# Moving the weight-block additions of the seven-product scheme from the vector engine to GpSimd

## Chip, cores and metric

The kernel runs on one core of one Trainium2 chip. The metric is the device time of one execution in microseconds (us).

## The reference, cut to what matters

Two network blocks work on 512 tokens of width 1024 in float32: a first block of two layers and a second block of one layer. What the change touches is the wide half of each feed-forward part (w_ff1 twice, then w_up):

```python
# first block, two layers
x = x + jnp.square(jax.nn.relu(h @ w_ff1[l])) @ w_ff2[l]     # 1024 -> 4096 -> 1024
# second block
f = jnp.square(jax.nn.relu(h @ w_up)) @ w_down
```

Around these stand pooling, latent attention and a recurrent branch (first block) and a state-space branch and dilated attention (second block); the change doesn't touch them.

## The kernel before

**Precision.** A float32 operand is split into a high and a low part in the fast matmul format: ACT copies the source to `hi`, DVE subtracts `lo = src - hi` (`split`). A product is then three matmuls (`mm3`): high x high, high x low, low x high.

**Seven products in place of eight.** For a pair of output tiles (128 columns each) of the wide projection, `up` (from L613 on) computes a 2 x 2 block product with seven block products in place of eight. A pair is called a unit here. Its weight blocks come from `wforms`: it loads two raw panels of 128 x 1024 (`r1`, `r2`, class W), whose halves are the blocks a11, a22, a12, a21 of 128 x 512, and forms four sums with the helper `add`: s1 = a22 + a21, s2 = s1 + a11, s3 = a11 + a21 and s2 + a12. Three blocks and the four sums are split by `both` into high and low (seven tiles of class W). The sums are tiles of class T, so in the trace the additions are `T<-W,W` (s1, s3) and `T<-T,W` (s2, s2 + a12). The activations' sums are made once per stage by `xforms`.

One product is four blocks of 128 rows times three matmuls of 256 columns, so a unit has 84 matmuls. `up` adds several products into the same PSUM tile `a`, and copies the tile out between them: product 0, copy, product 5, copy, product 6, copy, product 3, copy. Products 1, 4 and 2 go to two other PSUM tiles and fill the time of the copies. Afterwards DVE squares the positive part and the result is split.

**Loops.** `ffn` runs four units first; then for each of 24 panels of the down projection (each 24 matmuls of 512 columns) it does one unit after every second panel; the last eight panels follow. There are 16 units in each of the first block's two feed-forward stages and 14 in the second block's, 46 in all.

**What sets the order.** The kernel records every operation (`record`) with a duration from `cost`, and a list planner (`order`) lays all of them out over the five engines with the tile slots: 57 of class T, 16 of class W, 8 of PSUM. The instructions are then issued in this order, each engine in its own. Operations that write a W tile have 250 places of priority (`LEAD`). The planner may swap some ACT and DVE copies (`other`); it has no other engine for a GpSimd operation. Its prices for an addition of n elements a row are

```python
d = 65 + per * N + 60 * (ptr > 0)                             # vector, per = 1.05
d = 80 + (2.15 if m != "memset" else 0.9) * n(a[0])           # gpsimd
```

Since all instructions are issued from the one line of `emit`, L505 stands on every row of the profile; rows are told apart by engine, operation and tiles. `self.G` is needed for the activations' sums (a list, set in `mix1` and `out2`), and hides the proxy of the same name.

Of the kernel before, what the change touches and what calls it, by code (L numbers as in the profile page):

```python
# [11 lines left out]
ALU = mybir.AluOpType  # L12
# [49 lines left out]
class View:  # L62
    def __init__(self, tile, ops=()):
        self.tile, self.ops = tile, ops
# [122 lines left out]
class Recorder:  # L187
# [2 lines left out]

    def __init__(self, tc):
        self.tc, self.nc = tc, tc.nc
        self.V, self.A, self.G, self.E, self.S = (Proxy(self, e) for e in ("vector", "scalar", "gpsimd", "tensor", "sync"))
        self.ops = []


# [316 lines left out]
class Net(Recorder):  # L513
# [36 lines left out]
    def wforms(self, name, p):  # L550


        V, off, w = self.V, WOFF[name][0], 1024
        r1, r2 = self.new("W", w), self.new("W", w)
        for i, t in enumerate((r1, r2)):
            self.S.dma_start(t, bass.AP(tensor=self.wp.tensor, offset=off + (2 * p + i) * P * w, ap=[[w, P], [1, w]]))
        L, R = slice(0, T), slice(T, w)

        def both(x):
            hl = self.new("W", w, F32R)  # L560
            self.split(x, hl[:, L], hl[:, R])
            return hl[:, L], hl[:, R]

        def add(a, b):
            o = self.F()
            V.tensor_tensor(o, a, b, op=ALU.add)
            return o

        a11, a22, a12, a21 = r1[:, L], r1[:, R], r2[:, L], r2[:, R]
        f11, f12 = both(a11), both(a12)  # L570
        s1 = add(a22, a21)
        s2 = add(s1, a11)
        g2, g1 = both(s2), both(s1)
        s3 = add(a11, a21)
        g3, f22 = both(s3), both(a22)
        return f11, f12, both(add(s2, a12)), f22, g1, g2, g3
# [1192 lines left out]
```

## Time and profile before

| | us |
|---|---|
| median of 2 runs | 2489.48 (2489.26 to 2489.7) |
| the profiled execution's own time | 2488.91 |
| its span, first to last instruction | 2487.1 |

PE is TensorE's matmuls, PEld its weight loads, DVE the vector engine, ACT the scalar engine, POOL GpSimd, SP the engine that issues the transfers. A row of a group of instructions shows the engine, the operation, the tiles written and read, the shapes and the number, then the busy time, the mean length of one in ns, and how long the engine had been idle before them, with what ended that. The three feed-forward stages lie at about 326 to 720, 1026 to 1400 and 2112 to 2456 us of the span. TensorE's granted clock is at the full 2.4 GHz level in all three but for a few us.

### The profile page before, as it was taken

To read this page: it belongs to the slowest core of one execution; us is meant where nothing else is said; L and a number is where in the kernel's file an instruction comes from. 1 tells how busy PE (TensorE), PEld (TensorE's weight loads), DVE (VectorE), ACT (ScalarE), POOL (GpSimd) and SP (SyncE) were. 2 spreads that over 40 slices of the span, in tenths; PEclk is the share of its full clock that TensorE was granted. 3 is DMA by queue.
4 is the path that set the end of the run, shared out by engine and by line. 5 is a ranking of instruction groups with operands and counts; after the bars stand their busy time and mean duration, and the time that the engine had idled before them with its cause. 6 is when DMAs were issued, how large, how long until landed. Compare 5 with 4: busy or idle time off the path is not lost.

```text
span 2487.1 us, 35399 instructions
## 1 busy us (share of the span) xinstructions
PE 2462.5 (99%) x13822; PEld 2098.7 (84%) x13822; DVE 1911.1 (77%) x3451; ACT 1157.8 (47%) x2067; POOL 0.2 (0%) x4
## 2 busy tenths in 40 slices
PE   8999999999999999999999999999999999999997
PEld 7888889899888888899999977777778789998897
DVE  7868578777778785797776757588999887987775
ACT  5555355333345463553333334356755752743332
POOL 0000000000000000000000000000000000000000
PEclk9999999999999999999999999999999999999998
DMA  4222333333422223333333322244433452233321
GB/s 177 66 78 91 127 119 113 92 105 116 150 88 86 70 94 120 117 118 99 100 114 115 109 71 68 89 138 127 127 94 115 122 181 66 81 116 102 102 94 35
DMA packets 88599, 260.59 MB, mean 105 GB/s; under 512 B 10032, under 2 KB 13232, under 8 KB 88432
## 3 DMA queue, kind: packets, MB, share of 16 engines
q1 hardware_dynamic: 88432, 258.34, 32.6%
q8 instruction: 108, 1.77, 0.3%
q14 instruction: 59, 0.48, 0.1%
HBM read 245.59 MB, written 12.71 MB: 104 GB/s over the span
## 4 chain that ended last, share of the span: by engine, by line
PE 98%; DVE 1%; ACT 1%; issue 0%; DMA 0%; SPq 0%; ACTq 0%; DVEq 0%
PE P L505 98%; DVE T L505 1%; ACT T L505 1%; DMA T<-in_x_dram 0%; DVE W L505 0%; ACT W L505 0%; DVE S L505 0%; DVE xl L505 0%; SPq L505 0%; ACTq L1765 0%; ACT xh L505 0%; DVE xh L505 0%; DVEq L505 0%; ACTq L505 0%
## 5 line engine op out<-in xcount | busy, mean ns | idle before, releaser
L505 PE MATMUL P<-T,W 128*128 128x512 f32 (+1 forms) x5580 | 1100.2, 349 | 2.0 <-ACT T L505 2.0
L505 PE MATMUL P<-xh,W 128*128 128x512 f32 (+1 forms) x3912 | 1064.8, 351 | 8.1 <-DVE xh L505 6.3
L505 PEld LDWEIGHTS P<-T,W 128*128 128x128 f32 x5580 | 894.6, 188 | 142.5 <-ACT T L505 2.9
L505 PEld LDWEIGHTS P<-xh,W 128*128 128x128 f32 x3912 | 681.6, 189 | 114.1 <-issue 12.2
L505 PE MATMUL P<-xl,W 128*128 128x512 f32 (+1 forms) x1968 | 685.6, 351 | 1.2 <-DVE xl L505 1.2
L505 DVE TENSOR_TENSOR W<-W,W 128x1024 fp32r<-128x1024 f32 (+2 forms) x441 | 460.1, 1046 | 250.3 <-PE P L505 126.6
L505 ACT ACTIVATE W<-W 128x1024 fp32r<-128x1024 f32 (+2 forms) x424 | 386.8, 915 | 548.8 <-PE P L505 492.0
L505 PEld LDWEIGHTS P<-xl,W 128*128 128x128 f32 x1968 | 371.3, 189 | 55.6 <-issue 5.5
L505 DVE TENSOR_TENSOR T<-T,T 128x512 f32<-128x512 f32 (+6 forms) x636 | 378.9, 614 | 23.8 <-ACT T L505 14.1
L505 ACT ACTIVATE T<-T 128x512 fp32r<-128x512 f32 (+5 forms) x365 | 207.5, 578 | 250.2 <-DVE T L505 240.3
L505 PE MATMUL P<-T,T 128*128 128x256 f32 (+7 forms) x1536 | 278.0, 311 | 0.1
L505 PEld LDWEIGHTS P<-T,T 128*128 128x128 f32 (+2 forms) x1536 | 211.0, 184 | 39.8 <-issue 19.8
L505 ACT ACTIVATE T<-P 128x256 f32<-128x256 f32 (+7 forms) x295 | 136.6, 486 | 220.2 <-PE P L505 219.4
L505 DVE TENSOR_TENSOR T<-T,P 128x256 f32<-128x256 f32 (+2 forms) x328 | 166.7, 510 | 81.1 <-PE P L505 67.3
L505 DVE TENSOR_TENSOR T<-P,T 128x512 f32<-128x512 f32 (+5 forms) x224 | 131.1, 612 | 28.6 <-PE P L505 22.0
L505 ACT ACTIVATE W<-T 128x512 fp32r<-128x512 f32 x159 | 100.0, 631 | 110.1 <-PE P L505 96.3
L505 DVE TENSOR_TENSOR W<-T,W 128x512 fp32r<-128x512 f32 x184 | 124.0, 687 | 11.4 <-ACT W L505 9.5
L505 ACT ACTIVATE T<-T,T 128x128 f32<-128x128 f32 (+1 forms) x320 | 122.8, 455 | 7.9 <-DMA T<-fscr 6.7
L505 DVE SCALAR_TENSOR_TENSOR T<-T,P 128x512 f32<-128x512 f32 (+1 forms) x120 | 67.5, 575 | 38.8 <-PE P L505 27.3
L505 DVE COPY T<-P 128x256 f32<-128x256 f32 (+2 forms) x121 | 59.4, 493 | 30.1 <-PE P L505 28.6
L505 PE MATMUL P<-c,T 128*128 128x128 f32 (+1 forms) x436 | 75.1, 272 | 0.2 <-DVE T L505 0.2
L505 DVE SCALAR_TENSOR_TENSOR T<-P,half,T 128x510 f32<-128x510 f32 (+1 forms) x96 | 69.9, 743 | 0.4
(80 smaller groups left out, 1046.5 us busy)
## 6 DMA issues: line engine op xcount, KB each, us to landing
W<-in_w_dram SPq DMA_DIRECT2D x382, 512.0 KB, 3.6
T<-fscr SPq DMA_DIRECT2D x64, 256.0 KB, 4.6
T<-in_w_dram SPq DMA_DIRECT2D x24, 256.0 KB, 4.7
T<-in_x_dram SPq DMA_DIRECT2D x16, 256.0 KB, 5.6
rscr<-T SPq DMA_DIRECT2D x16, 256.0 KB, 3.9
T<-rscr SPq DMA_DIRECT2D x16, 256.0 KB, 5.2
W<-in_w_dram SPq DMA_DIRECT2D x10, 384.0 KB, 3.4
T<-in_c_dram SPq DMA_DIRECT2D x8, 256.0 KB, 4.0
```

The source lines that it names most:

```text
L505: self.out(o, getattr(getattr(self.nc, o.eng), o.meth)(*[res(a) for a in o.args], **{k: res(v) for k, v in o.kw.items()}))
```

## The change

The helper `add` of `wforms` records its addition on GpSimd in place of the vector engine. The GpSimd proxy gets the name `G_`, since `G` is taken over by the list named above. The planner is run with its price for GpSimd, so the order of instructions and the slots may change everywhere behind the first addition.

```diff
-        self.V, self.A, self.G, self.E, self.S = (Proxy(self, e) for e in ("vector", "scalar", "gpsimd", "tensor", "sync"))
+        self.V, self.A, self.G_, self.E, self.S = (Proxy(self, e) for e in ("vector", "scalar", "gpsimd", "tensor", "sync"))
...
         def add(a, b):
             o = self.F()
-            V.tensor_tensor(o, a, b, op=ALU.add)
+            self.G_.tensor_tensor(o, a, b, op=ALU.add)
             return o
```

## Rows read from the trace of the kernel before

**Rows 1.** The page, busy us (share of the span) x instructions of each engine.

```profile
PE 2462.5 (99%) x13822; PEld 2098.7 (84%) x13822; DVE 1911.1 (77%) x3451; ACT 1157.8 (47%) x2067; POOL 0.2 (0%) x4
```

**Rows 2.** Stretches: length, busy us (instructions) of PE, PEld, DVE, ACT, POOL; clock, DMA.

```profile
326.00:720.00 394.00, 394.00 (x2384) 349.75 (x2383) 303.12 (x497) 169.19 (x273) 0.00 (x0) 1.00 0.37 116
...
1026.00:1400.00 374.00, 374.00 (x2514) 343.42 (x2512) 293.01 (x542) 157.68 (x263) 0.00 (x0) 1.00 0.35 111
...
2112.00:2456.00 344.00, 340.20 (x2330) 313.99 (x2330) 265.77 (x494) 146.04 (x265) 0.00 (x0) 1.00 0.28 89
2456.00:2487.10 31.10, 18.14 (x129) 17.09 (x127) 17.97 (x61) 9.98 (x25) 0.00 (x0) 0.75 0.20 68
...
364.00:411.00 47.00, 47.00 (x385) 46.00 (x384) 44.51 (x84) 29.52 (x56) 0.00 (x0) 1.00 0.40 119
```

**Rows 3.** Waits of PE, 2112 to 2456 us: us in total, times, longest.

```profile
PE P L505 <- ACT T L505: 2.0, 1, 2.0
```

**Rows 4.** Groups of instructions on DVE, whole span: the additions, and the slowest operation.

```profile
L505 DVE TENSOR_TENSOR T<-T,W 128x512 f32<-128x512 f32 x92 | 62.9, 684 | 0.1
...
L505 DVE TENSOR_TENSOR T<-W,W 128x512 f32<-128x512 f32 x92 | 61.4, 683 | 0.6 <-DMA W<-in_w_dram 0.6
...
L505 DVE RECIPROCAL T<-T 128x512 f32<-128x512 f32 x4 | 13.4, 3340 | 0.0
```

**Rows 5.** Groups: additions from 326 to 396 us, 256-column matmuls from 326 to 409.6.

```profile
L505 DVE TENSOR_TENSOR T<-T,W 128x512 f32<-128x512 f32 x10 | 6.8, 684 | 0.0
L505 DVE TENSOR_TENSOR T<-W,W 128x512 f32<-128x512 f32 x10 | 6.6, 683 | 0.0
...
L505 PE MATMUL P<-xh,W 128*128 128x256 f32 x128 | 23.3, 277 | 0.0
L505 PE MATMUL P<-T,W 128*128 128x256 f32 x144 | 19.4, 283 | 0.0
L505 PE MATMUL P<-xl,W 128*128 128x256 f32 x64 | 17.6, 277 | 0.0
```

**Rows 6.** DVE: groups of 432.02 to 453.02 us, then single instructions (start, length).

```profile
L505 DVE TENSOR_TENSOR W<-T,W 128x512 fp32r<-128x512 f32 x4 | 2.7, 688 | 0.0
L505 DVE TENSOR_TENSOR W<-W,W 128x1024 fp32r<-128x1024 f32 x2 | 2.5, 1226 | 4.2 <-issue 3.9 <-PE P L505 0.4
L505 DVE TENSOR_TENSOR W<-W,W 128x512 fp32r<-128x512 f32 x3 | 2.1, 690 | 0.3 <-ACT W L505 0.2
...
L505 DVE TENSOR_TENSOR T<-T,T 128x512 fp32r<-128x512 f32 x2 | 1.4, 684 | 0.0
...
L505 DVE SCALAR_TENSOR_TENSOR T<-T 128x512 f32<-128x512 f32 x2 | 1.4, 683 | 0.0
...
395.06 0.69 DVE L505 TENSOR_TENSOR T<-T,W 128x512 f32<-128x512 f32 x1
...
436.52 0.41 DVE L505 COPY T<-P 128x256 f32<-128x256 f32 x1
...
439.53 0.42 DVE L505 COPY T<-P 128x256 f32<-128x256 f32 x1
...
448.88 0.69 DVE L505 TENSOR_TENSOR T<-T,W 128x512 f32<-128x512 f32 x1
```

**Rows 7.** PE in order of time: start us, length us, what, how many.

```profile
409.70 0.28 PE L505 MATMUL P<-xh,W 128*128 128x256 f32 x1
...
432.02 0.28 PE L505 MATMUL P<-xh,W 128*128 128x256 f32 x1
...
434.85 1.58 PE L505 MATMUL P<-T,W 128*128 128x256 f32 x12
...
437.64 1.59 PE L505 MATMUL P<-T,W 128*128 128x256 f32 x12
...
440.23 0.50 PE L505 MATMUL P<-T,W 128*128 128x512 f32 x2
...
453.02 0.28 PE L505 MATMUL P<-xh,W 128*128 128x256 f32 x1
```

## The prediction

> **What bounds the kernel.** I read the page's busy times first, then the stretches by stage, then what TensorE waited for, and at the end one period of the feed-forward loop instruction by instruction. PE is busy for 2462.5 of 2487.1 us [rows 1], so it has 24.6 us of idle time in the whole span. The stretches say where it lies: 13.0 us after 2456 us, 3.8 us in the third feed-forward stage (2112 to 2456), and none in the first two (326 to 720 and 1026 to 1400), where PE is busy for every microsecond [rows 2]; the remaining 7.8 us are outside these stages. The longest wait in the third stage is 2.0 us, for an ACT result [rows 3]. "Busy" is modelled, so I looked at the pace too: in the loop two products begin at 434.85 and 437.64 us [rows 7], and the 24 matmuls of 256 columns between these two points take 0.116 us each, with no hole. PE streams at its pace. All 184 additions that the change moves lie in these three stages, so what the vector engine saves there can shorten nothing but the 3.8 us. DVE is at 303.12 of 394, 293.01 of 374 and 265.77 of 344 us in them, 77 to 78%: loaded, and not what ends.
>
> **The change, part by part.**
>
> *Renaming the proxy.* It emits no instruction: nothing used the GpSimd proxy before (POOL holds four memsets, 0.2 us [rows 1]). Price nothing. The planner has no other engine for a GpSimd operation, so all 184 additions do go there; that the change does nothing is not a rival.
>
> *What leaves DVE.* There are 46 units of seven products (16, 16 and 14 per stage), each with four additions: 92 that read two W tiles (61.4 us) and 92 that read a T and a W tile (62.9 us) [rows 4]. That is 124.3 us, 0.676 us each. DVE falls to 303.12 - 64 x 0.676 = 259.9 us in the first stage, 293.01 - 43.3 = 249.7 in the second and 265.77 - 56 x 0.676 = 227.9 in the third. It saves time only where PE waited on DVE: at most the 3.8 us of the third stage, and those waits hang on the layer normalisation and on ACT; I take 0.
>
> *What comes to GpSimd.* No GpSimd arithmetic is in the trace of before. From below one addition costs no less than DVE's 0.676 us; from above the slowest element-wise operation of this size in the trace is the DVE reciprocal, 3.34 us [rows 4]. I take 1.18 us, which is what the kernel's own planner writes down for it (80 + 2.15 x 512 ns); it is nearer the adder's row than the reciprocal's, as an addition should be. Then GpSimd works 4 x 1.18 = 4.7 us in a unit. A unit with two panels of the down projection takes 21.0 us (units start at 432.02 and 453.02 [rows 7]), so GpSimd alone keeps up, even at 3.34 us (13.4 us).
>
> *Is the sum late?* What waits for an addition is the split of its result: the copy on ACT and the subtraction on DVE. Behind these stand, in order on their engines, the copies out of PSUM, and PE waits for those. So I count how early the additions are. From 326 to 396 us there are 20 of them, those of five units [rows 5], the last beginning at 395.06 [rows 6]; PE has by 409.6 done 128 + 144 + 64 = 336 matmuls of 256 columns, exactly four units of 84 [rows 5], and begins the fifth at 409.70 [rows 7]. The tightest unit thus has its last sum 409.70 - 395.75 = 13.95 us before its first product. In the loop it is more: the additions that end at 449.57 [rows 6] are for the unit after the one that starts at 453.02, at 474.0, 24 us later. Each unit's chain is three sums long at most, so at 1.18 us it is later by about 3 x (1.18 - 0.676) = 1.5 us and at 3.34 by 8.0 us. Both fit under 13.95. The new waits (GpSimd for the panel's transfer, GpSimd for its own last result, ACT and DVE for GpSimd) thus cost nothing as long as the lead stands; if a later order had no lead, a unit would lose 1.5 us, 46 x 1.5 = 69 us in all. The two raw panels stay in their slots 1.5 us longer. SyncE's issues are the same in number and size, no DMA is moved, and nothing else queues on POOL.
>
> *Do the two engines hinder each other?* Nearly all of DVE's work in the loop has both inputs in SBUF: in one period the splits and squares take 2.7 + 2.5 + 2.1 + 1.4 + 1.4 = 10.1 us [rows 6] beside the additions. No run here shows an addition of GpSimd beside them, so I bound it. Without hindrance the price is 0. If the two work strictly one after the other, 64 additions and DVE's rest need 259.9 + 64 x 1.18 = 335.4 us of the first stage's 394, 325.2 of 374 in the second and 294.0 of 344 in the third: still less than PE takes. The densest stretch, 364 to 411 us, where DVE has 44.51 of 47 us [rows 2], would need, with 16 additions for the four units that PE does in it, 44.51 - 16 x 0.68 + 16 x 1.18 = 52.5 us, 5.5 us too many, less than the lead of 13.95. So PE stays the bound at this price. The Trainium skill states this hindrance outright and it speaks against the change: "SBUF — State Buffer" (Who interferes with whom) says that a DVE instruction with two SBUF inputs and a GpSimd instruction that reads SBUF share a read interface, and that the second to be issued waits until the first is done. "GPSIMD Engine Reference" (Performance versus the Vector engine) measures such an addition at 4497 ns for 2048 elements against 2293 on DVE and advises DVE; a quarter, 1124 ns, would be an estimate for ours, and the three sums above would fall by 3 to 4 us each. No run here shows either yet.
>
> *The hand-offs.* A unit adds several products into one PSUM tile, with a copy out between them. After the product that begins at 434.85 [rows 7], DVE copies from 436.52 to 436.93 [rows 6] and PE goes on in that tile at 437.64 [rows 7]: 0.71 us to spare. The next copy ends at 439.95 [rows 6]; PE goes on with the second of the two matmuls of the row at 440.23, about 440.23 + 0.50 - 0.28 = 440.45 [rows 7]: 0.50 to spare. If DVE is held up by one addition, up to 1.18 us, PE loses up to 0.47 and 0.68 us. GpSimd is busy for 4.7 of 21 us, 22%; with the hold-up spread evenly from 0 to 1.18 the mean excess is 0.47 x 0.47 / 2.36 + 0.68 x 0.68 / 2.36 = 0.29 us, times 0.22 times 46 = 2.9 us. I take 2.9.
>
> *A new order.* The planner lays out every instruction anew with the new costs. PE's work stays the same, so I take 0 with a few us either way.
>
> **The sum.** 2487.1 + 2.9 = 2490.0 us of span; the profiled run took 2488.91 us, 1.8 us beyond its span, so 2491.8 us. The profiled run is 0.57 us under the median of 2489.48, so I round to 2492. Its own range is 2484 to 2500.
>
> **The rivals.**
> - *The hand-offs are hit every time.* If the plan repeats itself from period to period, an addition can stand in front of the copies in all of them: 46 x (0.47 + 0.68) = 52.9 us, 2542. For it: the loop's units follow each other in an even period of 21.0 us [rows 7], so a bad place comes back. Against it: DVE loses four instructions and already sits idle for 4.2 us ahead of one split in the period [rows 6]. The case covers 2500 to 2539.
> - *The vector engine becomes the bound, kernel slower.* It needs additions that hold DVE up for more than (394 - 259.9) / 64 = 2.10, (374 - 249.7) / 64 = 1.94 and (344 - 227.9) / 56 = 2.07 us. At 3.34 the stages would grow by 79.7, 89.5 and 70.9 us: 2489 + 240 = 2729. Below 1.94 us it costs nothing.
> - *A gain.* DVE's relief closes the 3.8 us of the third stage and the order turns out lucky: 2485, hardly under 2480. The last 13.0 us lie behind the last unit, in the layer normalisation of the output.
>
> **How the numbers follow.** Forecast 0.77 (2484 to 2500), hand-offs 0.12 (2500 to 2539), DVE bound 0.06 (2540 to 2729), gain 0.05 (2480 to 2485). A change of 2%, 49.8 us, is about what a measurement of this kernel can tell from none. Faster by more than that would need twice PE's idle time; I leave 0.01 for what I don't see, out of the gain's. Slower has the 0.06, the rest 0.93. A range of 2482 to 2512 leaves out the DVE bound, about half of the gain and two thirds of the hand-off case: 0.06 + 0.02 + 0.08 = 0.16.
>
> **What the profile after would show.** Right: POOL busy 184 x 1.2 = about 220 us, PE's busy time and pace unchanged, DVE's total at 1787 us or stretched by waits, no new wait of PE from 326 to 1400. The hand-off case: PE waiting on DVE T or ACT T inside the units, up to 0.7 us at a time, in every period. The DVE bound: additions of 2 us or more, DVE instructions longer than their 0.68 us, and stages longer than 394 and 374 us. My lead argument is wrong if PE waits for W tiles.

## The result and the profile after

| | before | after |
|---|---|---|
| median of 2 runs, us | 2489.48 | 2574.48 (2571.6 to 2577.36) |
| ratio to before, 95% interval | | 1.0344 [1.0326, 1.0362] |
| profiled run, us | 2488.91 | 2571.6 |
| its span, us | 2487.1 | 2569.8 |

The kernel became 3.4% slower. The span grew by 82.7 us; the prediction had said 2492 us and a range up to 2512.

The page of after, in the columns of [rows 1]:

```profile
PE 2496.8 (97%) x13822; PEld 2120.9 (83%) x13822; DVE 1953.9 (76%) x3303; ACT 1135.5 (44%) x2031; POOL 292.5 (11%) x188
```

The 184 additions are on POOL. DVE lost them and is nevertheless busier than before, 1953.9 against 1911.1 us [rows 1]. It has 3303 instructions, not 3451 - 184 = 3267: ACT lost 36 (2067 to 2031) and DVE got 36, so the planner moved copies onto the engine that it thought relieved. PE does the same 13822 matmuls; it is idle for 2569.8 - 2496.8 = 73.0 us, 48.4 more than the 24.6 of before.

The groups of instructions of after tell why DVE is busy (busy us, mean ns of one, then the idle time before them):

```profile
L505 POOL TENSOR_TENSOR T<-W,W 128x512 f32<-128x512 f32 x92 | 147.1, 1619 | 2125.7 <-DMA W<-in_w_dram 1136.3 <-ACT T L505 862.5 <-DVE T L505 77.2
...
L505 POOL TENSOR_TENSOR T<-T,W 128x512 f32<-128x512 f32 x92 | 146.9, 1597 | 35.1 <-DVE T L505 14.9 <-PE P L505 11.2 <-DVE W L505 5.7
...
L505 DVE TENSOR_TENSOR W<-T,W 128x512 fp32r<-128x512 f32 x184 | 150.6, 825 | 10.5 <-ACT W L505 8.8
...
L505 DVE TENSOR_TENSOR T<-T,P 128x256 f32<-128x256 f32 x218 | 89.8, 415 | 54.5 <-PE P L505 50.0 <-ACT T L505 2.6
```

An addition takes 1.61 us on GpSimd. The splits on DVE (W<-T,W, both inputs in SBUF) take 825 ns on average where they took 688 in [rows 6]. The operation with one input from PSUM (T<-T,P) takes 415 ns, as it did.

The list of one tile's instructions gives the spread of the additions (shortest, median, longest, ns):

```profile
L505 POOL TENSOR_TENSOR T<-W,W x92: 1282/1423/6641, 327.8 to 2448.2; 128x512 f32<-128x512 f32 x92
L505 POOL TENSOR_TENSOR T<-T,W x92: 1278/1616/2278, 330.5 to 2452.0; 128x512 f32<-128x512 f32 x92
```

Fourteen additions ran beside no DVE operation with two SBUF inputs, and these took 1.29 us each: that is the price with nothing in the way. The longest took 6.64 us (at 2210.66 us). During it DVE did nine operations in a row at their usual lengths, so here it was GpSimd that waited.

The stretches of after, start of each feed-forward stage and its loop, in the columns of [rows 2]:

```profile
326.00:440.00 114.00, 106.83 (x652) 96.15 (x651) 99.77 (x150) 55.82 (x100) 37.51 (x24) 0.96 0.29 90
440.00:740.00 300.00, 294.45 (x1716) 257.95 (x1715) 215.30 (x298) 101.38 (x152) 61.18 (x40) 0.99 0.38 118
1040.00:1160.00 120.00, 111.91 (x675) 100.34 (x674) 104.53 (x151) 55.03 (x101) 45.91 (x28) 0.96 0.32 102
1160.00:1450.00 290.00, 287.06 (x1932) 264.01 (x1932) 217.29 (x366) 105.48 (x171) 56.09 (x36) 0.99 0.33 105
2130.00:2260.00 130.00, 116.12 (x850) 108.83 (x849) 106.57 (x214) 59.89 (x130) 36.55 (x20) 0.96 0.24 78
2260.00:2500.00 240.00, 225.98 (x1386) 201.19 (x1385) 169.71 (x232) 80.05 (x126) 55.03 (x36) 0.98 0.29 92
```

PE now has holes in all of them: 7.2, 8.1 and 13.9 us in the starts (length less PE's busy time) and 5.6, 2.9 and 14.0 us in the loops, where before had none in the first two stages and 3.8 us in the third [rows 2]. In the third loop they come in every unit: PE waits for an ACT result at 2268.5, 2313.9, 2360.9, 2406.5 and 2453.5 us (1.8 to 2.1 us each) and for a DVE result at 2288.3, 2335.1, 2380.8 and 2427.7 (0.9 to 1.1).

Some waits in the whole span of after, of PE and, last, of ACT for a sum (us in total, times, longest):

```profile
PE P L505 <- ACT T L505: 25.3, 14, 2.8
PE P L505 <- DVE T L505: 13.1, 14, 2.2
PE P L505 <- DVE xl L505: 7.3, 7, 2.3
PE P L505 <- ACT W L505: 2.9, 1, 2.9
ACT W L505 <- POOL T L505: 6.3, 2, 3.9
```

PE waits for ACT and DVE results of class T (copies out of PSUM, activations) and for the low parts of the activations (xl). It waits for ACT's split of a weight panel once, 2.9 us at 2210 us; write_only and order_only below show the same wait, so it belongs to the new order. The sums come in time with two exceptions, both behind the addition of 6.64 us: ACT waits 6.3 us for them, and a wait of PE of 2.18 us follows at 2223 us.

**One hold-up, instruction by instruction.** The timeline of after from 395 to 404 us (start, length, engine, what; in brackets the idle time before it and what ended it):

```profile
395.11 3.00 POOL L505 TENSOR_TENSOR T<-W,W 128x512 f32<-128x512 f32 x2 [19.45 <-DMA W<-in_w_dram]
395.70 1.25 DVE L505 SCALAR_TENSOR_TENSOR T<-T 128x512 f32<-128x512 f32 x1
...
396.87 1.78 DVE L505 TENSOR_TENSOR W<-T,W 128x512 fp32r<-128x512 f32 x1
...
398.06 3.42 POOL L505 TENSOR_TENSOR T<-T,W 128x512 f32<-128x512 f32 x2
...
398.57 0.41 DVE L505 TENSOR_TENSOR T<-T,P 128x256 f32<-128x256 f32 x1
...
398.90 1.44 DVE L505 TENSOR_TENSOR T<-T,T 128x512 fp32r<-128x512 f32 x1
...
400.27 1.75 DVE L505 SCALAR_TENSOR_TENSOR T<-T 128x512 f32<-128x512 f32 x1
...
402.06 0.63 ACT L505 ACTIVATE T<-T 128x512 fp32r<-128x512 f32 x1 [3.44 <-DVE T L505]
...
402.60 0.61 ACT L505 ACTIVATE W<-W 128x512 fp32r<-128x512 f32 x1
...
403.12 0.36 ACT L505 ACTIVATE T<-P 128x256 f32<-128x256 f32 x1
...
403.53 1.83 PE L505 MATMUL P<-T,W 128*128 128x256 f32 x7 [2.81 <-ACT T L505]
```

This shows how the hold-up reaches PE. GpSimd does a unit's four additions in one burst, 395.11 to 401.48. In that time DVE does four operations with SBUF inputs. They take 1.25 + 1.78 + 1.44 + 1.75 = 6.2 us in place of 4 x 0.68 = 2.7; only the one that reads PSUM keeps its 0.41. Here the two engines take turns, one instruction each. DVE's square is late, so ACT stands for 3.44 us before its split of it; behind that split stand, in ACT's order, another split and the copy of a PSUM tile; and PE waits 2.81 us for that copy. The hold-up of a neighbour arrived two engines away, through the order of ACT's queue.

### The profile page after: what moved, and what is told of

Its sections match the earlier page's. It is cut to its first block, busy times and chain, and to the rows that moved or that the text cites. A ratio compares the mean times of both kernels' runs of the same rounds, so it can differ in the third digit from the quotient of the medians.

```text
span 2569.8 us, 35772 instructions
## 1 busy us (share of the span) xinstructions
PE 2496.8 (97%) x13822; PEld 2120.9 (83%) x13822; DVE 1953.9 (76%) x3303; ACT 1135.5 (44%) x2031; POOL 292.5 (11%) x188
## 3 DMA queue, kind: packets, MB, share of 16 engines
q8 instruction: 108, 1.77, 0.3%
## 4 chain that ended last, share of the span: by engine, by line
PE 51%; DVE 3%; issue 1%; ACT 1%; DMA 0%; POOL 0%; SPq 0%; ACTq 0%; DVEq 0%; POOLq 0%
PE P L505 51%; DVE W L505 2%; DVE T L505 2%; ACT T L505 0%; DMA W<-in_w_dram 0%; DVE S L505 0%; ACT W L505 0%; DVE xl L505 0%; POOL T L505 0%; SPq L505 0%; DVEq L505 0%; ACTq L1765 0%; ACTq L505 0%; POOLq L505 0%
## 5 line engine op out<-in xcount | busy, mean ns | idle before, releaser
L505 PE MATMUL P<-T,W 128*128 128x512 f32 (+1 forms) x5580 | 1117.3, 352 | 35.7 <-ACT T L505 25.3
L505 PE MATMUL P<-xh,W 128*128 128x512 f32 (+1 forms) x3912 | 1078.5, 354 | 11.6 <-DVE xh L505 6.7
L505 DVE TENSOR_TENSOR W<-W,W 128x1024 fp32r<-128x1024 f32 (+2 forms) x441 | 498.3, 1136 | 198.5 <-PE P L505 138.6
L505 ACT ACTIVATE W<-W 128x1024 fp32r<-128x1024 f32 (+2 forms) x400 | 367.9, 923 | 511.9 <-PE P L505 424.2
L505 DVE TENSOR_TENSOR T<-T,T 128x512 f32<-128x512 f32 (+6 forms) x636 | 399.1, 645 | 38.0 <-ACT T L505 28.1
L505 POOL TENSOR_TENSOR T<-W,W 128x512 f32<-128x512 f32 x92 | 147.1, 1619 | 2125.7 <-DMA W<-in_w_dram 1136.3
L505 ACT ACTIVATE T<-T 128x512 fp32r<-128x512 f32 (+6 forms) x364 | 207.1, 578 | 307.6 <-DVE T L505 298.3
L505 ACT ACTIVATE T<-P 128x256 f32<-128x256 f32 (+6 forms) x290 | 135.7, 490 | 246.1 <-PE P L505 244.6
L505 DVE TENSOR_TENSOR W<-T,W 128x512 fp32r<-128x512 f32 x184 | 150.6, 825 | 10.5 <-ACT W L505 8.8
L505 POOL TENSOR_TENSOR T<-T,W 128x512 f32<-128x512 f32 x92 | 146.9, 1597 | 35.1 <-DVE T L505 14.9
```

The lines of the kernel that those rows point to most:

```text
L505: self.out(o, getattr(getattr(self.nc, o.eng), o.meth)(*[res(a) for a in o.args], **{k: res(v) for k, v in o.kw.items()}))
```

## The experiments

Two theories stood at the start. Theory 1: GpSimd's reads of SBUF hold up DVE's operations with two SBUF inputs. Its rival: the sums come later, and the chain behind them with them. A third cause, the new order of all instructions, had to be split off. All ratios are to runs of the kernel before beside it, with 95% intervals.

**After's order, GpSimd only writes.** Each addition becomes three writes of its result tile, which last about as long (1.6 us) and read nothing. The kernel leaves out the sums, so its output is not the network's.

```diff
+                if o.eng == "gpsimd":
+                    for _ in range(3):
+                        self.nc.gpsimd.memset(res(o.args[0]), 0.0)
+                    continue
```

> The changed kernel with each addition on GpSimd replaced by three memsets of its result in a row (about as long, but they read nothing); the sums are left out, and weight blocks made of them are zero. Theory 1 (reads through a shared interface hold up the vector engine): vector lengths back at 0.69 us, 2487 to 2500 us. Rival (the additions come later, whatever they read): still 2550 us and more, PE waiting for ACT and DVE results.

Measured: 2495.07 us, 1.0026 [1.0014, 1.0037]. Its page in the columns of [rows 1], its groups, and its dense stretch in the columns of [rows 2]:

```profile
PE 2467.6 (99%) x13822; PEld 2101.5 (84%) x13822; DVE 1824.8 (73%) x3303; ACT 1138.2 (46%) x2031; POOL 287.0 (12%) x556
...
L507 POOL MEMSET T<- 128x512 f32 x552 | 286.8, 530 | 2074.5 <-ACT W L509 804.2 <-PE P L509 671.1 <-DVE T L509 340.4
...
L509 DVE TENSOR_TENSOR W<-T,W 128x512 fp32r<-128x512 f32 x184 | 125.5, 688 | 11.0 <-ACT W L509 7.0
```

```profile
364.00:411.00 47.00, 47.00 (x387) 46.12 (x386) 39.98 (x78) 27.78 (x50) 15.41 (x31) 1.00 0.34 107
```

GpSimd is about as busy as in after (287.0 against 292.5 us), yet the splits on DVE are back at 688 ns, PE has no hole in the dense stretch, and the span is 7.8 us over before's. So 2569.8 - 2494.9 = 74.9 of the 82.7 us go away with the reading. Writes don't need the raw panels either, so GpSimd no longer waits for these, and this run alone doesn't separate the reading from sums that come later. The waits of after do: ACT waits 6.3 us in all for sums, DVE never. Lateness falls as the main cause.

The two runs also give the price on DVE. It executes the same 3303 instructions, and they keep it busy for 1953.9 us in after and 1824.8 here: 129.1 us of hold-ups, 0.70 us for each of the 184 additions. DVE had spent 0.676 us on each when it did them itself, so it won nothing.

**After's order, additions back on DVE.**

```diff
-                self.out(o, getattr(getattr(self.nc, o.eng), o.meth)(...
+                self.out(o, getattr(getattr(self.nc, "vector" if o.eng == "gpsimd" else o.eng), o.meth)(...
```

> The order and slots that the planner made for the change, with the 184 additions issued on the vector engine at their places. Theory 1 (GpSimd's reads of SBUF hold up the vector engine): the order is harmless, 2487 to 2500 us, vector splits of 512 columns back at 0.69 us, no waits of PE inside the units. Rival (the new order itself is bad): about 2570 us with the same waits of PE.

Measured: 2521.72 us, 1.0131 [1.0102, 1.0160]; neither expectation had this. A group, and the wait of PE that is largest in total:

```profile
L505 DVE TENSOR_TENSOR W<-T,W 128x512 fp32r<-128x512 f32 x184 | 125.0, 686 | 4.9 <-ACT W L505 3.4
```

```profile
PE P L505 <- DVE T L505: 16.0, 17, 1.9
```

DVE's lengths are normal, and GpSimd does nothing. The new order itself is 32.8 us of span worse when DVE has to do the additions. In the run above the same order cost 7.8 us with DVE free of them. This fits a planner that has spent DVE's freed time, on the 36 copies taken from ACT among other things, and left no room for hold-ups. Which of its choices matters was not separated.

**Before's order, additions issued on GpSimd.** The plan is made as before; only the engine that issues the marked additions changes.

```diff
-                self.out(o, getattr(getattr(self.nc, o.eng), o.meth)(...
+                self.out(o, getattr(getattr(self.nc, "gpsimd" if o.moved else o.eng), o.meth)(...
...
             V.tensor_tensor(o, a, b, op=ALU.add)
+            self.ops[-1].moved = True
```

> The order of the kernel before, untouched, with the 184 additions issued on GpSimd. Theory 1 (hindrance): splits of 512 columns lengthened to 0.8 us and more, PE idle, 2530 to 2620 us. Rival (the new order): 2487 to 2500 us. If longer chains of additions alone do it, the additions here have no planned room, so it is slow under that theory too.

Measured: 2533.45 us, 1.0178 [1.0149, 1.0208], in the range of theory 1. Start and loop of the first stage, then the loops of the second and third, in the columns of [rows 2]:

```profile
326.00:440.00 114.00, 105.64 (x654) 94.51 (x653) 98.99 (x141) 57.76 (x108) 43.21 (x28) 0.97 0.33 104
440.00:740.00 300.00, 298.62 (x1757) 262.41 (x1756) 208.85 (x306) 110.84 (x166) 53.98 (x37) 1.00 0.35 113
...
1160.00:1430.00 270.00, 268.29 (x1795) 245.48 (x1794) 201.97 (x337) 98.05 (x156) 55.26 (x35) 1.00 0.33 108
...
2250.00:2480.00 230.00, 229.50 (x1475) 206.75 (x1474) 165.60 (x235) 78.83 (x121) 57.27 (x36) 1.00 0.30 97
```

In before's order the loops lose 1.4 + 1.7 + 0.5 = 3.6 us, against 22.5 in after's. The first start loses 8.4 us, as in after (7.2). So the starts lose with the reads in either order, and most of after's loss in the loops comes only with the new order. That order's loops have no room even without a read: in order_only, with the additions on DVE, they lose 9.2 us, in write_only none.

**Before's order and additions on DVE, with GpSimd reading beside them.** GpSimd repeats each addition in two halves of 256 columns into a scratch tile that nobody reads, so no sum can be late. To make room for that tile, this kernel and the next have 30 slots of class S in place of 48; PE's matmuls keep their order.

```diff
+                if o.moved:
+                    for h in HALVES:
+                        self.nc.gpsimd.tensor_tensor(self.dummy, *[res(a)[:, h] for a in o.args[1:]], op=ALU.add)
```

> The kernel before in its own order, additions on the vector engine; beside it GpSimd repeats every addition, in two halves of 256 columns, into a scratch tile that nobody reads. Nothing waits for a GpSimd result except the release of the panels' slots. If GpSimd's reads hold up the vector engine: vector splits of 512 columns above 0.69 us, PE waits, 2510 to 2600 us. Rival (what costs is that the sums come later): 2487 to 2495 us.

Measured: 2544.93 us, 1.023 [1.020, 1.026], as theory 1 expected. Groups:

```profile
L508 DVE TENSOR_TENSOR T<-T,W 128x512 f32<-128x512 f32 x92 | 87.8, 954 | 0.1
...
L508 DVE TENSOR_TENSOR W<-T,W 128x512 fp32r<-128x512 f32 x184 | 150.8, 832 | 18.3 <-ACT W L508 17.1
...
L508 DVE TENSOR_TENSOR T<-T,P 128x256 f32<-128x256 f32 x218 | 90.0, 415 | 49.3 <-PE P L508 47.1 <-ACT T L508 1.5
```

Nothing was moved and nothing waits for GpSimd's results, and the kernel is 55.2 us of span slower. (ACT and DVE do wait, 30.8 us in all, until GpSimd has read a tile whose slot they are to fill; how much of the loss that makes was not separated.) Again the two-input operations stretch (684 to 954, 688 to 832 ns) and the one with a PSUM input doesn't.

**Bursts spread out.** Before's order with the additions on GpSimd, and six writes of a scratch tile behind each, so that four additions don't follow each other at once.

```diff
+                if o.moved:
+                    self.nc.gpsimd.tensor_tensor(*[res(a) for a in o.args], op=ALU.add)
+                    for _ in range(6):
+                        self.nc.gpsimd.memset(self.dummy, 0.0)
+                    continue
```

> The order of the kernel before with the additions on GpSimd, as in old_order (2533 us), but each addition is followed on GpSimd by six memsets of a scratch tile of 256 columns, so that the four additions of a unit no longer follow each other at once. If several hold-ups in a row are what reaches PE: 2490 to 2515 us, with the vector splits lengthened as much in sum as in old_order. Rival (only the sum of the hold-ups counts): 2525 to 2545 us.

Measured: 2532.79 us, 1.0181 [1.0152, 1.0211], the same as without the gaps. Two of its waits:

```profile
DVE W L510 <- POOL T L506: 22.0, 9, 4.5
ACT W L510 <- POOL T L506: 19.7, 9, 3.8
```

This leaves the question of bursts open. DVE is busy for 1905.8 us, 27.2 less than in old_order with the same 3267 instructions, so the hold-ups did shrink. But the writes make the sums late: ACT and DVE wait 63.2 us in all for GpSimd, where they waited 5.3 in old_order. PE's holes move with that, from the starts to the loops: 11.7 us in the loops against 3.6. Equal times here are two losses that happen to be alike.

**Additions of the first four units of each stage (in the third stage of two, units 2 and 3) on DVE, planned anew.**

```diff
-            self.G_.tensor_tensor(o, a, b, op=ALU.add)
+            (V if p < 4 else self.G_).tensor_tensor(o, a, b, op=ALU.add)
```

> The additions of the first four units of each stage (units 0 to 3, in the third stage 2 and 3) stay on the vector engine, 144 of 184 go to GpSimd. If the loss is even over the additions: 2489 + 85 x 144 / 184 = 2556 us. If it comes from the dense starts of the stages, where the trace of after loses some 14 us each in the first two: 2525 to 2545 us. If all of it comes from the starts: under 2500 us.

Measured: 2529.70 us, 1.0163 [1.0134, 1.0193], in the range that the dense starts were given. 144 of 184 additions are still on GpSimd and about half of the loss is gone.

**The same split in before's order.** Only the other units' 144 additions on GpSimd, and then only those 40 of the first units.

```diff
+            self.ops[-1].moved = p >= 4      # and, in the second kernel, p < 4
```

> The order of the kernel before; only the 144 additions of units 4 and later go to GpSimd, those of the first four units of a stage stay on the vector engine. In old_order nearly all of the loss of 44 us lies in the dense starts of the stages, where the vector engine has almost no idle time. If lack of vector time there is the cause: 2492 to 2508 us. If the loss is even over the additions: 2489 + 44 x 144 / 184 = 2523 us.

> The complement: the order of the kernel before, only the 40 additions of units 0 to 3 (2 and 3 in the third stage) go to GpSimd. If the dense starts are the cause: 2512 to 2530 us. If the loss is even over the additions: 2489 + 44 x 40 / 184 = 2499 us.

Measured: 2510.67 us, 1.0088 [1.0071, 1.0105], and 2508.81 us, 1.0083 [1.0068, 1.0098]. The dense start of the first stage in the first kernel, then in the second:

```profile
364.00:425.00 61.00, 57.32 (x461) 55.52 (x460) 54.83 (x88) 34.00 (x64) 14.11 (x9) 1.00 0.35 109
```

```profile
364.00:425.00 61.00, 56.72 (x427) 54.72 (x426) 53.25 (x89) 34.63 (x65) 6.00 (x4) 0.94 0.35 104
```

I had expected the first four units to carry nearly all of it. Both runs lie between their two expectations: these units carry 19.9 us of span and the other units 20.7, together 40.6 of old_order's 43.7. The first row shows why: nine additions of later units are done in the dense stretch too, since the planner forms them ahead. Over before, PE's holes in the starts of this kernel are 11.9 us, those in its loops 2.1. The loss hangs on the place in time, not on the unit's number. Per addition the first four units cost 19.9 / 40 = 0.50 us, the others 20.7 / 144 = 0.14.

**A planner that knows only the price.** The planner's price of an addition on GpSimd is raised from 1.18 to 80 + 3.0 x 512 ns = 1.62 us.

```diff
-            d = 80 + (2.15 if m != "memset" else 0.9) * n(a[0])
+            d = 80 + (3.0 if m != "memset" else 0.9) * n(a[0])
```

> The changed kernel with the planner's price for a GpSimd addition at 80 + 3.0 x 512 = 1616 ns, what it measures in the trace of after (1.61 us), and nothing else. If the unplanned hold-ups of the vector engine are the cause: still 2530 to 2590 us. Rival (the planner only took GpSimd for too fast): 2487 to 2505 us.

Measured: 2548.28 us, 1.0244 [1.0213, 1.0274]. A right price helps, and leaves some 60 of 85 us.

**A planner that knows the exclusion.** `shared` is true for the additions on GpSimd and for DVE operations with two SBUF inputs (and plain copies); two such are never planned at the same time. The price is 80 + 2.5 x 512 ns.

```diff
-                est = efree[e]
+                est = max(efree[e], port[0]) if shared(o, e) else efree[e]
...
+            if shared(o, e):
+                port[0] = o.end
```

> The changed kernel with a planner that knows the hindrance: GpSimd additions and vector operations with two SBUF inputs (and plain copies) are never planned at the same time, price of an addition 80 + 2.5 x 512 = 1360 ns. By the sums of the prediction the work still fits under PE's in every stage. If the loss comes from hold-ups that the order did not allow for: 2487 to 2505 us. Rival (the hindrance can't be planned away): 2530 us and more.

Measured: 2520.90 us, 1.0134 [1.0104, 1.0163], above the 2487 to 2505 of theory 1 and below the 2530 of its rival. Start and loop of the first stage, then of the third:

```profile
326.00:440.00 114.00, 109.08 (x692) 97.55 (x691) 97.46 (x148) 60.39 (x110) 45.48 (x28) 1.00 0.33 102
440.00:735.00 295.00, 295.00 (x1732) 259.66 (x1731) 206.06 (x294) 116.92 (x175) 55.49 (x36) 1.00 0.36 116
...
2110.00:2260.00 150.00, 137.65 (x968) 128.08 (x967) 126.12 (x236) 75.19 (x156) 51.77 (x24) 0.95 0.23 78
2260.00:2480.00 220.00, 220.00 (x1440) 199.97 (x1439) 145.26 (x214) 76.81 (x123) 45.43 (x32) 1.00 0.27 94
```

The loops lose nothing any more, the second stage's included, with GpSimd as busy as ever. The starts still lose 4.9, 5.9 and 12.3 us, the last with before's 3.8 in it: there, this planner found no order that makes room for it.

**The same planner, first four units on DVE.** The last edit and the `p < 4` of above together.

> The planner that knows the hindrance (plan_knows, 2521 us), with the additions of the first four units of a stage on the vector engine. If dense starts and unplanned hold-ups in the loops are the two causes, both are gone: 2487 to 2500 us, PE without waits from 326 us on but for the third stage. If something else is left: 2510 us and more. Neither theory has it faster than the kernel before by more than 4 us, since PE is the bound.

Measured: 2514.72 us, 1.0103 [1.0088, 1.0118], above the 2487 to 2500 expected: something else was left. The dense start of its first stage:

```profile
364.00:425.00 61.00, 55.25 (x431) 53.33 (x430) 52.57 (x83) 32.39 (x59) 13.47 (x8) 0.97 0.30 92
```

The loss is again in the starts alone (PE's holes in the three loops are 0.2 us). As in old_from4, keeping four units on DVE doesn't keep GpSimd out of the dense stretch: eight additions of later units run in it. No version beat the kernel before, nor was one to be expected where PE has 24.6 us of idle time in all.

## Why the prediction was wrong

*What bounds the kernel: right.* PE has no use for DVE's saving, and no kernel came out faster. DMA and SP were no part of it.

*The price of an addition: too low, and not what decided.* 1.18 us was taken; 1.29 is measured with nothing in the way, 1.61 as the mean with the waiting for DVE. With 1.61 the prediction's own stage sum for strict turns would be 259.9 + 64 x 1.61 = 363 of 394 us. It still fits, and the kernel still lost 83 us. The condition of the second rival (DVE becomes the bound), a hold-up of 1.94 us per addition averaged over a stage, was never met either: it was 0.70. The measured time does lie in the range given to that rival, 2540 to 2729, and two of its signs came (longer DVE instructions, longer stages), but by another path. A sum over a stage could not see this loss.

*The hindrance: right in kind.* The prediction named the mechanism, and the rows bear it out: splits of 0.69 us last up to 1.80. Matched one by one with write_only, no DVE operation with a PSUM input is more than 13 ns longer, and ACT's splits (W<-T) keep their 630 ns. DVE's copies with a single SBUF input stretch too (CAST W<-T, 0.43 us, up to 1.54), which the prediction had not counted. The rule that the Trainium skill gives in "SBUF — State Buffer" (Who interferes with whom), DVE's two SBUF inputs against a GpSimd instruction that reads, agrees with what the operations with two inputs show; so does its remark that GpSimd instructions which only write don't hinder these (688 ns in write_only). Which of the two waits isn't told by the start alone: at 2210.66 us nine DVE operations that began after the addition were done before it. The estimate from the Trainium skill's "GPSIMD Engine Reference" (Performance versus the Vector engine), 1124 ns, lies below the shortest addition, 1278 ns; the measurement decides.

*The lead: right but for two sums.* ACT waits 6.3 us for sums, both in the start of the third stage, for which the prediction had counted no lead. PE never waits for the split of a sum.

*The dense stretch: the step that failed.* The prediction found 5.5 us too many in 364 to 411 us and dismissed them with "less than the lead of 13.95". That lead belongs to the sums. DVE's other work in the stretch, the low parts of the activations for the same stage and the copies out of PSUM, has no such lead where PE waits for it. The stretches of after, in the columns of [rows 2], show it:

```profile
345.00:364.00 19.00, 19.00 (x84) 15.39 (x83) 18.81 (x27) 9.59 (x19) 8.34 (x6) 1.00 0.36 120
364.00:380.00 16.00, 11.94 (x63) 10.87 (x61) 15.07 (x23) 7.93 (x16) 5.73 (x4) 0.79 0.20 66
```

From 345 to 364 us DVE is busy for 18.81 of 19 us with 27 instructions, where before did 36 in 17.61 us; it has become full while PE still runs. From 364 to 380 PE stands for 4.1 us. The timeline at that place:

```profile
372.52 3.13 POOL L505 TENSOR_TENSOR T<-T,W 128x512 f32<-128x512 f32 x2
...
372.76 1.77 DVE L505 TENSOR_TENSOR W<-T,W 128x512 fp32r<-128x512 f32 x1
...
374.45 1.75 DVE L505 TENSOR_TENSOR xl<-T,xh 128x512 fp32r<-128x512 f32 x1
...
376.26 0.57 PE L505 MATMUL P<-xl,W 128*128 128x256 f32 x1 [2.31 <-DVE xl L505]
```

Two DVE operations in a row take 1.77 and 1.75 us beside a pair of additions, the second makes xl, and PE waits 2.31 us for it. The stretch could have been priced: with DVE at 44.51 of 47 us [rows 2], 16 additions fit only below (47 - 44.51 + 16 x 0.68) / 16 = 0.84 us each, under every price but the lowest bound. At the measured 1.61 the prediction's sum gives 44.51 - 10.9 + 25.8 = 59.4, 12.4 us too many. By the count of PE's matmuls, after has at 440 us done 652 from 326 us on, which before had at about 426.4: some 13.5 us behind. That the two agree is chance. In after only eight additions run from 364 to 411 us (before's DVE does 15 there, the prediction took 16) and DVE is busy for 39.9 of these 47, since the engines wait for each other once the chain has slipped, and an addition does not cost DVE its whole length. Matched one by one with write_only, DVE's instructions from 326 to 440 us are 20.7 us longer in after, 0.86 us for each of the 24 additions there, where DVE had won 0.68; and of the 13.5 us, 7.2 are holes of PE and some are the clock's (last section).

*The hand-offs: near in one run, far off in the new order.* 2.9 us were forecast for all loops; old_order lost 3.6, though reads_too, in the same order, lost 8.1. After lost 22.5: this term of the sum was mis-sized. The term counted one hold-up on a DVE copy, up to 1.18 us against margins of 0.71 and 0.50. The timeline shows several in one burst, and the copy that PE waits for on ACT, behind a split that waits for DVE. The rival "hit every time" (2542) had the sign and part of the place, and its point came nearest. In the third loop every unit is hit, as it said, with waits of 0.9 to 2.1 us and not of up to 0.7; it had nothing for the starts.

*A new order, "0 with a few us either way": wrong.* In the new order the reads cost 74.9 us of span (after against write_only); in the old one the whole move costs 43.7. The planner put work on DVE as if it had become free, and did not know that its two engines exclude each other. That this is what made the loops lose is shown by plan_knows: the same planner with the exclusion has loops without holes. With the price alone (price_only) they still lose some 7 us.

*Where the 82.7 us lie.* By the count of PE's matmuls about 44 us are lost in the three starts and 38 in the loops, 22 of these in the third. By kind, PE's idle time is 48.4 of them. The clock takes part (last section), about 21. Some 13 are left, which lie within PE's modelled busy time and were not resolved; order_only, at before's clock, has the same 13 us (PE busy 2475.6 against 2462.5), write_only, in the same order, 5.1.

## What to carry to other kernels

In this kernel, additions moved to GpSimd did not leave DVE, since they read SBUF while DVE worked with two SBUF inputs: each cost DVE 0.70 us of hold-up in place of 0.68 of work, and 1.61 us on GpSimd. Budget such a move on the densest stretch of DVE, not on a stage's mean, and ask of a lead whose it is: the moved work's lead doesn't cover its neighbours. A planner that lays out such a move has to know the exclusion; the one here filled the time that looked free and left no room for the hold-ups.

## What was not expected of the hardware

TensorE's granted clock fell where PE had waited. Stretches of after, in the columns of [rows 2]:

```profile
376.40:379.40 3.00, 3.00 (x14) 3.00 (x15) 2.28 (x5) 1.49 (x3) 0.00 (x0) 0.50 0.00 0
380.00:383.00 3.00, 3.00 (x28) 3.00 (x27) 2.39 (x6) 2.03 (x5) 0.00 (x0) 1.00 0.03 5
```

In before the clock is at 1.00, the 2.4 GHz level, from 364 to 411 us [rows 2]. In after PE's wait of 2.31 us ends at 376.26; behind it the clock is at 0.50, the 1.2 GHz level, and PE does 14 matmuls in 3 us, where it does 28 in the next row. The same follows the wait of 2.81 us that ends at 403.53 (15 matmuls from 403.7 to 406.7 us, clock 0.50), and the waits of 0.68 and 1.04 us just before 369 us (0.50 from 369.6 to 372.6). Over the span the mean is 0.988 in after and 0.996 in before: 2569.8 x 0.012 - 2487.1 x 0.004 = 31 - 10 = about 21 us. Such waits thus cost PE more than their own length.

The profile counts the waiting for the other engine as part of an instruction, as DVE's 1.78 us for a split show. A rising "busy" of an engine with less to do is how such an exclusion looks on the page.
